# A hybrid encoder step: keys of two head groups, and the queries of one, projected turned, and rotated by a shuffle of partitions

## The chip, the cores and the metric

The kernel runs on one core of one Trainium2 chip. The metric is the time of one execution in device microseconds (us). Five instruction queues work side by side and meet by semaphores: TensorE (PE: matmuls and transposes, with weight loads shown as PEld), VectorE (DVE), ScalarE (ACT), GpSimd (POOL) and SyncE (SP, which issues the DMA transfers). SBUF and PSUM are the on-chip memories; PSUM's eight banks take what PE writes. Times are the median of several runs; a profile is one execution apart.

## The reference

One layer of a streaming encoder works on a prompt of 512 rows and on 32 new rows ("sample") of another sequence with caches. Rows are 1024 wide.

```
z = rmsnorm(x) @ w_in              # 3880 columns: qa ka va ga | qb kb vb gb | qm gm | qi ki wi
A: 6 heads x 64, attention over own chunk and 8 before, learned relative bias
B: 6 heads x 64, qb and kb rotated: [x1 cos - x2 sin, x2 cos + x1 sin] over halves of a head;
   an indexer (qi, ki, wi) picks the keys of each query, attention over those
M: 4 heads x 64, attention into 256 memory rows (their keys and values projected from mem)
x + concat(oA silu(ga), oB silu(gb), oM silu(gm)) @ w_out, then rmsnorm
```

Besides the two outputs, the new keys and values of A and B (prompt and sample), B's rotated indexer key and the memory's keys and values are returned. All is float32.

## The kernel before

Matmuls of 32-bit precision are made of three faster products: each operand is split into a high part, rounded (names ending in h: `xTh`, `wh`), and a low part, the rest (`xTl`, `wl`); high x high, low x high and high x low are summed in PSUM. The input stands turned in SBUF, model dimension on partitions, prompt and sample side by side (`xTh`, `xTl`: 8 pieces k of 128 x 544 columns).

Weights come in pieces by DMA (`raw`), ACT rounds a piece (`wh`) and POOL subtracts (`wl`). Two forms of projection use them. `group_n` ("natural") holds 128 rows of x as weights on PE and streams up to 384 columns of `wh`/`wl`: four row tiles, 8 k, 3 products; the result has rows on partitions. The 32 sample rows are not in it: `w_sample` computes them apart from the unsplit weights, eight matmuls of 32-row output for a projection, and `sample_rows` adds four partial sums on DVE. `group_t` ("turned") holds 128 weight columns and streams x in two halves of 272 columns (512 prompt rows and 32 sample rows); the result has features on partitions and needs no extra work for sample.

In the kernel before, A's keys (ka), A's values (va), B's keys (kb), queries (qb) and values (vb) are natural; A's queries, the memory's queries and the gates are turned. B's rotation is done on natural rows by `rope`: DVE multiplies by sine with the halves exchanged, DVE multiplies by cosine, DVE or POOL adds. Sample's rows get `rope_s`. Attention needs keys and queries turned: `turned_pair` transposes four 128 x 128 tiles on PE for a pair of heads, and `parts` splits the result into high and low. In `sample`, new keys are transposed and copied behind the cached ones.

The scores of a pair of heads and some row tiles form a unit: scores on PE, minimum and bias on DVE, exponential on ACT, normalization, transposes of the weights on PE (`turn`), and the product with the values (`mix`). A's and M's units come before B's.

The order of each engine's instructions is written when the program is built: a planner (`Line`) records every operation with an assumed cost, keeps a clock for each engine, and lets tasks issue when their inputs are due. PE's order is the backbone: the projections, in the order of `EARLY` and `LATE`, then the output projection; attention, sample and the selection of keys are put between their matmuls. All operations are recorded through one helper, so nearly every row of the profile has its line, L405. `SURE`, `LAG` and `SLACK` are the planner's margins and factor on costs; `WV` names the weight pieces that DVE splits in POOL's place. On SP, weights, caches, results stored and tables stand in one queue.

Of the kernel before, what the change touches and what calls it, by code (L numbers as in the profile page):

```python
# [10 lines left out]
F32 = mybir.dt.float32  # L11
# [9 lines left out]
T = 32  # L21
# [14 lines left out]
WV = (0, 1, 2, 3)  # L36
START = "xxxtwwwwrrrrrwmmrr"
SURE = 1.0
SLACK = 1.1
HOLD = 3.0  # L40
LAG = 0.2
# [3 lines left out]
EARLY = ("ka", "va", "mk", "mv", "qa0", "qa1", "ga0", "qa2", "ga1", "ga2", "qm0", "gm0", "qm1", "gm1")  # L45
LATE = ("gb0", "kb", "qb", "vb", "gb1", "gb2")
# [387 lines left out]
def hybrid_step(ctx: ExitStack, tc: tile.TileContext, a: dict):  # L434
# [73 lines left out]
    ka = va = ysS = None  # L508
# [69 lines left out]
    NATURAL = {"i": (QI, 296), "ka": (KA, 384), "va": (VA, 384), "kb": (KB, 384), "qb": (QB, 384), "vb": (VB, 384)}  # L578
    TURNED = {"qa": QA, "ga": GA, "qm": QM, "gm": GM, "gb": GB}
# [25 lines left out]
    def w_load():  # L605
        party = {p + j for _, p, _ in parties for j in range(NK // 2)} | set(range(n_in, n_in + 16))
        for i, (w, k, nk, lo, hi) in enumerate(w_list):
# [4 lines left out]
            if i == n_in + 12:  # L612

                yield from line.wait(lambda: units[-1].pair.q is not None)
# [87 lines left out]
    def sample_rows(nm, n, p):  # L702
        yield line.at(p)
        if nm in ("kb", "vb"):
            yield from line.wait(lambda: 0 in over)
        full = (cp.tile([P, 384], F32, tag={"kb": "kaS", "vb": "vaS"}.get(nm, nm + "S"), name=nm + "S") if nm != "i"
# [11 lines left out]
        yield from line.wait(lambda: NT in normed and (nm not in ("kb", "qb") or "qb" in over))  # L718
# [4 lines left out]
        if nm not in ("kb", "qb"):  # L723
            news[nm] = full if nm[0] == "v" else out
        if nm in ("kb", "qb"):
            yield from rope_s(out, T, 6, 64, ctab["cos64S"], ctab["sin64S"])
            news[nm] = out
# [219 lines left out]
    for nm in ("cos32", "sin32", "cos64", "sin64"):  # L947
        d = int(nm[3:])
        tp = ro if d == 64 else ix
        ctab[nm] = tp.tile([P, NT, d], F32, name=nm)  # L950
        ctab[nm + "S"] = tp.tile([T, d], F32, name=nm + "S")

    def load_tables(d):

        for nm in (f"cos{d}", f"sin{d}"):
            DMA.dma_start(ctab[nm], a[nm][0:S].rearrange("(t p) d -> p t d", p=P))
            DMA.dma_start(ctab[nm + "S"], a[nm][S:N])

        def scale():
            yield from line.wait(lambda: count["scored"] > 1)  # L960
            for t in range(NT):
                yield from line.wait(lambda: t in normed)
                for nm in (f"cos{d}", f"sin{d}"):
                    x = ctab[nm][:, t, :]
                    yield line.at(x, rs[:, t:t + 1])
                    G.tensor_scalar(x, x, rs[:, t:t + 1], None, op0=ALU.mult)
                over[d, t] = True

        if d == 64:
            line.spawn(scale())  # L970

    def rope(out, src, rows, nh, d, cos, sin, eng=None):
# [3 lines left out]
        t1 = ro.tile([P, 384], F32, tag="rt", name="rt")  # L976
# [8 lines left out]
    def rope_s(x, rows, nh, d, cos, sin):  # L985

        h2 = d // 2
        yield from room()
        p = bank()
        t1 = p[:rows, 0:nh * d]  # L990
        v2 = x.rearrange("p (h s d) -> p h s d", s=2, d=h2)[:, :, ::-1, :]
        sv = sin.rearrange("p (s d) -> p s d", s=2).unsqueeze(1).broadcast_to([rows, nh, 2, h2])
        yield line.idle(V)
        V.tensor_tensor(t1.rearrange("p (h s d) -> p h s d", s=2, d=h2), v2, sv, op=ALU.mult)
        yield line.idle(V)
        xv = x.rearrange("p (h d) -> p h d", d=d)
        V.tensor_tensor(xv, xv, cos.unsqueeze(1).broadcast_to([rows, nh, d]), op=ALU.mult)
        yield line.idle(V)
        V.tensor_tensor(x, t1, x, op=ALU.add)
        give(p)  # L1000


# [260 lines left out]
    def sample_choice():  # L1263
# [46 lines left out]
        yield from line.wait(lambda: count["scored"] >= len(TILES) and "qb" in over)  # L1310
# [38 lines left out]
    def project(nm, dst, out_p, out_s):  # L1349
        def done(t, acc):  # L1350
            if nm in ("kb", "qb"):
                rope(dst[:, t, :].rearrange("p (h d) -> p h d", d=64), acc[:, 0:384], P, 6, 64,
                     ctab["cos64"][:, t, :], ctab["sin64"][:, t, :])
            else:
                scaled(dst[:, t, :], acc[:, 0:384], rs[:, t:t + 1])

        def finish():
            if out_p:
                store_rows(a[out_p], dst)
                store_new(a[out_s], nm)  # L1360
            over[nm] = True

        return group_n(xTh, xTl, 384, NT, done, finish, 0, x_done)

# [55 lines left out]
    def projections(order):  # L1420
        nonlocal ka, va
        for nm in order:
            m = "abm".find(nm[1])
            if nm[0] in "qg" and nm != "qb" and gates[m] is None:
# [10 lines left out]
            elif nm[0] == "q" and nm != "qb":  # L1435
                line.until(lambda: "rb" in over)
                line.run(queries(nm))
            elif nm[0] == "m":
                line.run(memory(nm, mk if nm == "mk" else mv, f"new_mem_{nm[1]}_p"))
            else:  # L1440
                if nm not in natural:

                    line.until(lambda: NT - 1 in normed if nm[1] == "a" else (2 if nm == "kb" else 0) in over)
                    natural[nm] = cp.tile([P, NT, 384], F32, tag=nm, name=nm)
                    ka, va = (natural.get(n) for n in ("ka", "va"))
                of = f"new_{nm[1]}_{nm[0]}"
                line.run(project(nm, natural[nm], None if nm == "qb" else of + "_p", of + "_s"))


    def sample(mix, nh, nb, kt, cv, qT, kn, vn, pts, zin):  # L1450
# [5 lines left out]
        nk = nn + (T if kn is not None else 0)  # L1456
        if kn is not None:
            yield line.sure(kn)
            yield from room()
            p = bank()  # L1460
            for hp, k in enumerate(kt):
                PE.transpose(p[:, hp * T:(hp + 1) * T], kn[:, hp * P:(hp + 1) * P], ident[:T, :T])
            for hp, k in enumerate(kt):
                either(k[:, nn:nk], p[:, hp * T:(hp + 1) * T])
            give(p)
        yield line.sure(qT, *kt)
# [4 lines left out]
        for g0 in range(0, nh, 4):  # L1471
# [12 lines left out]
            def scores_of():  # L1484
                scs = [bank() for _ in cuts]
                for sc, (k0, n) in zip(scs, cuts):
                    for j, h in enumerate(hs):
                        r = 64 * (h % 2)
                        PE.matmul(sc[T * j:T * j + T, 0:n], qT[r:r + 64, h // 2, -T:], kt[h // 2][r:r + 64, k0:k0 + n],
# [131 lines left out]
    def sample_a():  # L1621
        yield from line.wait(lambda: all(n in over for n in ("qa0", "qa1", "qa2", "mk", "mv")) and "ka" in news and "va" in news)
        kt = cp.tile([P, 3, N], F32, tag="gate1", name="keysA")
        DMA.dma_start(kt[:, :, 0:S], a["cache_a_k"].rearrange("(m p) n -> p m n", p=P))
# [8 lines left out]
        yield from sample(0, 6, 4, [kt[:, m, :] for m in range(3)], cav, queried[0], news["ka"], news["va"],  # L1633
# [18 lines left out]
    def attention():  # L1652
        nonlocal ap, oax
        yield from line.wait(lambda: all(n in over for n in ("index", "index_s", "ka", "va")) and NT + NM // P in normed)
# [25 lines left out]
    def split_q(src, scale, sub):  # L1680
        return parts("q", src, S, scale, sub)

# [35 lines left out]

    SCORES = 9
# [163 lines left out]
    def biases():  # L1883
# [15 lines left out]
        yield from line.wait(lambda: count["mixed"] >= 3 * len(TILES))  # L1899
        oT[1] = cp.tile([P, 3, S], F32R, tag="ka", name="oBh"), cp.tile([P, 3, S], F32R, tag="va", name="oBl")  # L1900

    for hp in range(3):
        pair = Pair(0, hp, lambda hp=hp: both(split_q(queried[0][:, hp, 0:S], 1.0, G), keys_of(ka, hp)), lambda: va)
        pair.needs = lambda hp=hp: 2 * hp + 1 in nbs and f"qa{hp}" in over
# [221 lines left out]
```

## Time and profile before

| | |
|---|---|
| median of 3 runs (lowest to highest) | 352.41 us (352.28 to 352.43) |
| span of the profiled execution, first to last instruction | 350.8 us |
| PE busy | 342.6 us, 2748 matmuls |
| PE weight loads | 300.2 us |
| DVE / ACT / POOL busy | 277.5 / 224.2 / 174.3 us |
| mean granted TensorE clock | 0.996 |
| DMA | 46.31 MB |

A timeline row has the start in us, the duration in us, engine, line, operation, output<-inputs, shape, count and, in brackets, idle time before it with what ended it. Matmuls overlap in the pipeline, so a row's duration is longer than the step to the next row's start. Matmuls that read unsplit 32-bit data are recorded twice (x16 for 8). A row of groups has count | busy us, mean ns | idle time before and what ended it. A transfer's row has the count, KB each and median us from issue to landing.

### The profile page before, as it was taken

The page shows a single profiled execution, that of the slowest core. Times are in us where ns is not written, and L with a number is a line of the kernel's source. Part 1 is how long each engine was busy: PE and PEld are TensorE (multiplying, and loading weights), DVE is VectorE, ACT ScalarE, POOL GpSimd, SP SyncE. Part 2 cuts the span into 40 slices and gives each one's busy share as a digit, 9 for nine tenths or more (in the row PEclk, how much of TensorE's full clock was granted, in tenths as well). Part 3 has the DMA queues.
Part 4 walks back from the last instruction along what each step waited for, and adds up shares of the span by engine and source line. Part 5 has one row for each costly group of instructions (what it writes and reads, how often), then busy time and mean ns, then how long its engine had stood idle before and what let it go on. Part 6 is the DMA issues. An engine that isn't in the chain of part 4 may idle for free.

```text
span 350.8 us, 7580 instructions
## 1 busy us (share of the span) xinstructions
PE 342.6 (98%) x2748; PEld 300.2 (86%) x2748; DVE 277.5 (79%) x700; ACT 224.2 (64%) x536; POOL 174.3 (50%) x195
## 2 busy tenths in 40 slices
PE   8999999999999999999999999999999999999992
PEld 8979989989999998898898899899986777676882
DVE  3765768699889999997999945798996899674743
ACT  5759678898564876894757427413795786472542
POOL 3468264475554585255634473744471465215622
PEclk9999999999999999999999999999999999999998
DMA  7999542456538251343231232232372537300033
GB/s 230 323 360 354 134 140 75 143 162 152 151 92 296 66 144 39 78 127 88 76 91 45 93 124 58 60 93 98 95 284 92 180 106 265 114 0 2 0 111 143
DMA packets 39604, 46.31 MB, mean 132 GB/s; under 512 B 5360, under 2 KB 32624, under 8 KB 39568
## 3 DMA queue, kind: packets, MB, share of 16 engines
q1 hardware_dynamic: 39568, 45.85, 42.0%
q8 instruction: 21, 0.34, 0.4%
q14 instruction: 15, 0.12, 0.1%
HBM read 39.67 MB, written 6.16 MB: 131 GB/s over the span
## 4 chain that ended last, share of the span: by engine, by line
PE 95%; DVE 1%; ACT 1%; issue 1%; POOLq 0%; POOL 0%; ACTq 0%; DVEq 0%
PE bank L405 95%; DVE rot L405 1%; DVE xr L405 0%; ACT junkS L405 0%; DVE rt L405 0%; ACT wh L405 0%; ACT sq L405 0%; POOLq L2114 0%; POOL xr L405 0%; ACT bf_ok L405 0%; ACT k L405 0%; POOL ss L405 0%; ACT wI L405 0%; DVE ones L405 0%; ACTq L405 0%
## 5 line engine op out<-in xcount | busy, mean ns | idle before, releaser
L405 POOL TENSOR_TENSOR wl<-raw,wh 128x512 fp32r<-128x512 f32 (+1 forms) x69 | 104.5, 1523 | 79.9 <-ACT wh L405 68.2
L405 ACT ACTIVATE wh<-raw 128x512 fp32r<-128x512 f32 (+2 forms) x77 | 50.7, 662 | 23.4 <-PE bank L405 12.0
L405 PE MATMUL bank<-wh,xTh 128*128 128x384 f32 (+1 forms) x184 | 61.2, 347 | 0.2 <-ACT k L405 0.2
L405 PE MATMUL bank<-wl,xTh 128*128 128x384 f32 (+1 forms) x184 | 58.8, 334 | 0.0
L405 PE MATMUL bank<-wh,xTl 128*128 128x384 f32 (+1 forms) x184 | 58.5, 332 | 0.0
L405 ACT ACTIVATE z<-z,st 128x256 f32<-128x256 f32 (+3 forms) x80 | 42.4, 553 | 18.9 <-DVE st L405 18.7
L405 PE MATMUL bank<-xTh,wh 128*128 128x272 f32 x208 | 46.3, 303 | 0.0
L405 PE MATMUL bank<-xTl,wh 128*128 128x272 f32 x208 | 43.0, 288 | 0.0
L405 PE MATMUL bank<-xTh,wl 128*128 128x272 f32 x208 | 42.9, 288 | 0.0
L405 PEld LDWEIGHTS bank<-wh,xTh 128*128 128x128 f32 x184 | 34.1, 190 | 1.8 <-ACT wI L405 0.6
L405 PEld LDWEIGHTS bank<-xTh,wh 128*128 128x128 f32 x208 | 32.7, 189 | 2.7 <-issue 1.8
L405 PEld LDWEIGHTS bank<-wl,xTh 128*128 128x128 f32 x184 | 34.1, 190 | 0.0
L405 PEld LDWEIGHTS bank<-wh,xTl 128*128 128x128 f32 x184 | 33.9, 189 | 0.1
L405 PEld LDWEIGHTS bank<-xTl,wh 128*128 128x128 f32 x208 | 32.6, 188 | 0.0
L405 PEld LDWEIGHTS bank<-xTh,wl 128*128 128x128 f32 x208 | 32.6, 189 | 0.0
L405 DVE MAX8 m<-ysel 128x8 f32<-128x256 f32 (+2 forms) x48 | 26.5, 552 | 0.1
L405 DVE MATCH_REPLACE8 ysel<-m,ysel 128x256 f32<-128x256 f32 (+2 forms) x48 | 26.0, 542 | 0.0
L405 PE MATMUL bank<-ident,z 128*128 128x128 f32 (+1 forms) x162 | 24.8, 274 | 0.0
L405 ACT ACTIVATE junkS<-ysS,bi 128x1056 int8<-128x1056 f32 x16 | 18.8, 1172 | 6.8 <-DVE bi L405 5.7
L405 PEld LDWEIGHTS bank<-ident,z 128*128 128x128 f32 (+1 forms) x162 | 18.6, 140 | 5.1 <-issue 1.6
L405 ACT COPY z<-bank 128x512 f32<-128x512 f32 (+2 forms) x31 | 15.7, 520 | 10.2 <-PE bank L405 8.5
L405 DVE SCALAR_TENSOR_TENSOR ysel<-r,wI,ysel 128x256 f32<-128x256 f32 (+2 forms) x21 | 19.7, 938 | 2.4 <-ACT r L405 1.8
(299 smaller groups left out, 784.1 us busy)
## 6 DMA issues: line engine op xcount, KB each, us to landing
raw<-in_w_in_dram SPq DMA_DIRECT2D x20, 384.0 KB, 3.7
raw<-in_w_in_dram SPq DMA_DIRECT2D x26, 256.0 KB, 2.9
raw<-in_w_out_dram SPq DMA_DIRECT2D x16, 256.0 KB, 3.6
xr<-in_x_t_dram SPq DMA_DIRECT2D x8, 272.0 KB, 4.4
nat<-in_x_prompt_dram SPq DMA_DIRECT2D x4, 512.0 KB, 7.7
raw<-in_w_mem_kv_dram SPq DMA_DIRECT2D x8, 256.0 KB, 2.7
xr<-in_x_prompt_dram SPq DMA_DIRECT2D x4, 512.0 KB, 3.3
out_dram<-xr SPq DMA_DIRECT2D x4, 512.0 KB, 2.6
```

Source lines behind the costliest of these rows:

```text
L405: return fn(*args, **kw)
```

## The change

A's keys, B's keys and B's queries are projected turned, in three parts of 128 columns each (`ka0` to `ka2`, `kb0`, `qb0` and so on), prompt and sample together. `keys` takes a part out of PSUM: A's keys are multiplied by the rows' norms on DVE. B's go through `rope_t`: a shuffle within groups of 32 partitions exchanges the halves that a rotation mixes (the columns of `w_in` and the cached keys of B are put into the matching order on the host), DVE multiplies by cosine, DVE or POOL by sine, POOL adds. The tables of cosine and sine are now turned, 128 x 544, with the norms multiplied in on POOL. The transposes of ka, kb and qb, and those of sample's new keys and queries, are gone: `split_of` splits the turned tiles directly, and `sample` reads the new keys from their own tile. The extra matmuls for sample's rows remain for the indexer, va and vb. New keys are stored turned and put back by the host when it cuts the results apart. `EARLY` and `LATE` have a new order, and the planner's numbers differ.

```diff
-WV = (0, 1, 2, 3)
+WV = (0, 1, 2, 3, 5, 7)
-SURE = 1.0
-SLACK = 1.1
+SURE = 1.3
+SLACK = 1.05
-LAG = 0.2
+LAG = 0.3
-EARLY = ("ka", "va", "mk", "mv", "qa0", "qa1", "ga0", "qa2", "ga1", "ga2", "qm0", "gm0", "qm1", "gm1")
-LATE = ("gb0", "kb", "qb", "vb", "gb1", "gb2")
+EARLY = ("va", "ka0", "ka1", "mk", "ka2", "mv", "qa0", "qa1", "ga0", "qa2", "ga1", "ga2", "qm0", "gm0", "qm1", "gm1")
+LATE = ("gb0", "gb1", "gb2", "kb0", "qb0", "kb1", "qb1", "kb2", "qb2", "vb")
+SWAP = [(i + 16) % 32 for i in range(32)]
...
+    def rope_t(out, p, sl):
+        t = ro.tile([P, N // 2], F32, tag="rq", name="rq", bufs=2)
+        V.stream_shuffle(t, p, SWAP)
+        V.tensor_tensor(out, p, ctab["cos64"][:, sl], op=ALU.mult)
+        def rest():
+            least(out, V, G).tensor_tensor(t, t, ctab["sin64"][:, sl], op=ALU.mult)
+            yield line.at(t, out) - 0.2
+            G.tensor_tensor(out, t, out, op=ALU.add)
+        return rest()
...
+        def done(sl, p):
+            x = xT[:, i, sl]
+            if nm[1] == "b":
+                turned(x, p, sl)
             else:
+                V.tensor_tensor(x, p, rb[:, sl], op=ALU.mult)
+                ready(x)
+        return group_t(done)
...
-            for hp, k in enumerate(kt):
-                PE.transpose(p[:, hp * T:(hp + 1) * T], kn[:, hp * P:(hp + 1) * P], ident[:T, :T])
...
-        pair = Pair(1, hp, lambda hp=hp: both(turned_pair(natural["qb"], hp, lambda p, w: split_q(p, -0.125, V)), keys_of(natural["kb"], hp)),
+        pair = Pair(1, hp, lambda hp=hp: both(split_of(natural["qb"][:, hp, 0:S], -0.125, V, "q"),
+                                              split_of(natural["kb"][:, hp, 0:S], 1.0, G, "k")), lambda: natural["vb"])
```

Three places show how the order of instructions moves. First PE, where the first unit of B is prepared. Before (`ident,qb` and `ident,kb` are the transposes, `k,q` and its kin the scores, `xT` with `w` a turned projection, here of a gate):

```order
L405 MATMUL bank<-kl,q 128x256 x2
L405 MATMUL bank<-ident,qb 128x128 x4
L405 MATMUL bank<-ident,kb 128x128 x4
L405 MATMUL bank<-xTh_81,wh 128x272 x2
L405 MATMUL bank<-xTl_83,wh 128x272 x2
```

In the change the scores of that unit stand straight between the matmuls of a projection, which is now one of B's own keys and queries:

```order
L406 MATMUL bank<-xTh_82,wl 128x272 x2
L406 MATMUL bank<-k,q 128x128 x2
L406 MATMUL bank<-k,ql 128x128 x2
L406 MATMUL bank<-kl,q 128x128 x2
L406 MATMUL bank<-k,q 128x256 x2
L406 MATMUL bank<-k,ql 128x256 x2
L406 MATMUL bank<-kl,q 128x256 x2
L406 MATMUL bank<-xTh_82,wh 128x272 x2
```

The transposes are gone, and B's first scores have moved ahead of the end of B's projections.

Second POOL, in B's key and query parts. Before (`wl` is a weight split, `kb<-rt,kb` the last step of a rotation):

```order
L405 TENSOR_TENSOR ql<-queried,q 128x512
L405 TENSOR_TENSOR kb<-rt,kb 128x384
L405 TENSOR_TENSOR oAl<-o,oAh 128x384
L405 TENSOR_TENSOR kb<-rt,kb 128x384
L405 TENSOR_TENSOR wl<-raw,wh 128x768 x2
```

In the change (`rq` holds the shuffled half, `sin_123` the sine table, `kl` the low part of a pair's keys):

```order
L406 TENSOR_TENSOR wl<-raw,wh 128x512 x3
L406 TENSOR_TENSOR rq<-rq,sin_123 128x272
L406 TENSOR_TENSOR kb<-rq,kb 128x272
L406 TENSOR_TENSOR wl<-raw,wh 128x512
L406 TENSOR_TENSOR kb<-rq,kb 128x272
L406 TENSOR_TENSOR wl<-raw,wh 128x512
L406 TENSOR_TENSOR oMl<-o,oMh 128x512
L406 TENSOR_TENSOR wl<-raw,wh 128x512
L406 TENSOR_TENSOR rq<-rq,sin_123 128x272
L406 TENSOR_TENSOR qb<-rq,qb 128x272 x2
L406 TENSOR_TENSOR wl<-raw,wh 128x512
L406 TENSOR_TENSOR kl<-kb,k 128x512
```

The three splits in the first row are the second piece of `kb0` and both of `qb0`. All additions of the rotation, and sines, now stand between the weight splits of the following parts.

Third PE, where B's values, the last projection, end in the change (`oA`, `oM` belong to the output projection, `raw,oS` to sample's output, `z,vb` is the first product with B's values):

```order
L406 MATMUL bank<-wl,xTh_82 128x384
L406 MATMUL bank<-wh,oAh 128x512
L406 MATMUL bank<-wh,oAl 128x512
L406 MATMUL bank<-wl,oAh 128x512
...
L406 MATMUL bank<-wl,oMh 128x512
L406 MATMUL bank<-raw,oS 32x512 x4
L406 MATMUL bank<-z,vb 64x128 x6
```

Before, two gate projections stood between B's values and the output projection.

More of the change, by code (lines that the diff above doesn't have):

```diff
@@ L612, in w_load @@
             if i == n_in + 12:
-                yield from line.wait(lambda: units[-1].pair.q is not None)
+                yield from line.wait(lambda: units[-1].pair.q is not None and "newB" in over)
                 for tag, n, dtype in (("qb", 3, F32), ("kb", 2, F32R)):
@@ L717, in sample_rows @@
         give(p)
-        yield from line.wait(lambda: NT in normed and (nm not in ("kb", "qb") or "qb" in over))
+        yield from line.wait(lambda: NT in normed)
         yield max(line.at(rs[0:T, NT:NT + 1]), line.at(out) - 0.2)
@@ L722, in sample_rows @@
         V.tensor_scalar(out, out, rs[0:T, NT:NT + 1], None, op0=ALU.mult)
[L723 to L727, printed above, removed]
+        news[nm] = full if nm[0] == "v" else out
     def tokens(acc, xh, xl, w, c, t, c0, c1, first, last):
@@ L1455, in sample @@
         nn = nb * P
[L1456 to L1460, printed above, removed]
[L1461 to L1466 removed]
+        nk = nn + (T if vn is not None else 0)
+        yield line.sure(qT, *kt, *([kn] if kn is not None else []))
         yield from room(3)
@@ L1621, in sample_a @@
     def sample_a():
-        yield from line.wait(lambda: all(n in over for n in ("qa0", "qa1", "qa2", "mk", "mv")) and "ka" in news and "va" in news)
-        kt = cp.tile([P, 3, N], F32, tag="gate1", name="keysA")
-        DMA.dma_start(kt[:, :, 0:S], a["cache_a_k"].rearrange("(m p) n -> p m n", p=P))
+        yield from line.wait(lambda: all(n in over for n in ("qa0", "qa1", "qa2", "ka0", "ka1", "ka2", "mk", "mv")) and "va" in news)
+        kt = cp.tile([P, 3, S], F32, tag="gate1", name="keysA")
+        DMA.dma_start(kt, a["cache_a_k"].rearrange("(m p) n -> p m n", p=P))
         t = cp.tile([P, 3 * S], F32, tag="qb", name="tmpA")
@@ L1653, in attention @@
         nonlocal ap, oax
-        yield from line.wait(lambda: all(n in over for n in ("index", "index_s", "ka", "va")) and NT + NM // P in normed)
+        yield from line.wait(lambda: all(n in over for n in ("index", "index_s", "ka0", "va")) and NT + NM // P in normed)
         ipx.close()
@@ L1919, in hybrid_step @@
     projections(LATE)
-    line.until(lambda: 1 in gated and all(n in over and n in news for n in ("kb", "qb", "vb")))
+    line.until(lambda: 1 in gated and all(n in over for n in BK + ("vb",)) and "vb" in news)
     rox.close()
@@ L1951, in sample_b @@
         line.spawn(values())
-        yield from line.wait(lambda: "choice" in over and all(n in news for n in ("kb", "qb", "vb")))
+        yield from line.wait(lambda: "choice" in over and "vb" in news)
         z2 = cp.tile([P, NKS], F32, tag="rank", name="z2")
         V.tensor_copy(z2[0:2 * T], ysS[0:2 * T])
-        yield from room()
-        qbS = sp.tile([P, 3, T], F32, name="qbS")
-        p = bank()
-        for hp in range(3):
-            PE.transpose(p[:, hp * T:(hp + 1) * T], news["qb"][:, hp * P:(hp + 1) * P], ident[:T, :T])
-        rounded(qbS, p[:, 0:3 * T].rearrange("p (m c) -> p m c", m=3), -0.125)
-        give(p)
-        yield from sample(1, 6, 8, [t[:, 0:NKS] for t in kt], cbv, qbS, news["kb"], news["vb"],
-                          pts + [kt[2][:, NKS:]],
+        yield from sample(1, 6, 8, [t[:, 0:PAST] for t in kt], cbv, qbS, kbS, news["vb"],
+                          pts + [kt[2][:, PAST:]],
                           lambda g0, rows: z2 if g0 else ysS)
```

174 lines of the change are left out of this document (103 added, 71 removed).

## Prediction

> **What bounds the kernel now.** I read the page's busy shares first, then the chain that ended last, then what TensorE (PE) waited for.
>
> ```profile
> span 350.8 us, 7580 instructions
> PE 342.6 (98%) x2748; PEld 300.2 (86%) x2748; DVE 277.5 (79%) x700; ACT 224.2 (64%) x536; POOL 174.3 (50%) x195
> ...
> PE 95%; DVE 1%; ACT 1%; issue 1%; POOLq 0%; POOL 0%; ACTq 0%; DVEq 0%
> ...
> PE bank L405 <- DVE ones L405: 1.0, 1, 1.0
> PE bank L405 <- ACT bf_ok L405: 0.7, 1, 0.7
> PE bank L405 <- ACT k L405: 0.2, 1, 0.2
> ```
>
> The first line is one profiled execution; the median of the timed runs is 352.41 us, 1.6 us more, and I carry that difference over unchanged. PE is busy for 98% of the span, 95% of the last chain is PE, and PE's waits after the start come to 0.9 us. Busy PE is not PE at its peak, but with hardly a wait the spacing of its instructions is the time. So I price the change by start-to-start intervals on PE, and then ask whether the other engines still keep up.
>
> **The change part by part.**
>
> *Projections.* The timeline of PE, first and last row of a stretch of 384-wide matmuls with nothing between, then the same for 272-wide ones (a row of x2 is two matmuls with one weight tile):
>
> ```profile
> 33.12 0.34 PE L405 MATMUL bank<-wh,xTh 128*128 128x384 f32 x1
> ...
> 42.90 0.34 PE L405 MATMUL bank<-wl,xTh 128*128 128x384 f32 x1
> ...
> 247.30 0.42 PE L405 MATMUL bank<-xTl,wh 128*128 128x272 f32 x2
> ...
> 255.05 0.41 PE L405 MATMUL bank<-xTh,wl 128*128 128x272 f32 x2
> ```
>
> Between the first two lie 56 intervals: 9.78 / 56 = 0.1746 us each. Between the other two lie 62: 7.75 / 62 = 0.125 us. A projection of 384 columns was 4 row tiles x 8 k x 3 products = 96 matmuls, 16.76 us. Turned, with sample's 32 rows along, it is 3 parts x 8 k x 3 products x 2 halves = 144 matmuls, 18.0 us. Three projections turn (A's keys, B's keys, B's queries): **+3.72 us**.
>
> The Trainium skill, "TensorE: Matmul & The Clock Gate", section "Back-to-back issue gap", speaks against such a trade: it gives a sustained spacing of about 81 ns for 128 columns and 131 ns for 512, because weight load and matmul both count. On a straight line between these, an estimate, 272 columns take 100 ns and 384 take 114 ns, a projection goes from 11.0 to 14.4 us, and three cost +10.2 us in place of +3.72. The rows above disagree (125 and 174.6 ns) and are the very two shapes, so the measurement decides.
>
> *What goes from PE.*
>
> ```profile
> 44.16 1.50 PE L405 MATMUL bank<-raw,xF 128*32 128x384 f32 x16
> 45.58 0.82 PE L405 MATMUL bank<-identR,stk 32*128 32x32 f32 x8
> ...
> 126.82 0.66 PE L405 MATMUL bank<-ident,ka 128*128 128x128 f32 x4
> 127.23 0.50 PE L405 MATMUL bank<-xTh,wh 128*128 128x272 f32 x2
> ...
> 246.11 0.66 PE L405 MATMUL bank<-ident,qb 128*128 128x128 f32 x4
> 246.60 0.60 PE L405 MATMUL bank<-ident,kb 128*128 128x128 f32 x4
> 246.96 0.50 PE L405 MATMUL bank<-xTh,wh 128*128 128x272 f32 x2
> ...
> 260.44 0.37 PE L405 MATMUL bank<-ident,qbS 32*128 32x32 f32 x3
> 260.65 0.34 PE L405 MATMUL bank<-ident,kbS 32*128 32x32 f32 x3
> 260.93 0.50 PE L405 MATMUL bank<-wh,oAh 128*128 128x512 f32 x1
> ```
>
> Sample's own rows of a projection take 45.58 - 44.16 = 1.42 us; three such groups go: **-4.26**. A's keys are turned back in three groups of four transposes, 0.41 us each; B's queries and keys in three pairs of groups, 0.85 us a pair: 1.23 + 2.55 = **-3.78**. Sample's small transposes: 0.49 for B's two, half of it for A's keys: **-0.74**. The sample's scores against its 32 new keys stay as many and as wide; only their tile changes.
>
> *Re-entries.* A run of projections that starts again after something else is slow on its first step: 246.96 to 247.30 is 0.34 us where two matmuls take 0.25. The output projection does the same:
>
> ```profile
> 269.91 0.48 PE L405 MATMUL bank<-wh,oAh 128*128 128x512 f32 x1
> 270.23 0.40 PE L405 MATMUL bank<-wh,oAl 128*128 128x512 f32 x1
> 270.47 0.40 PE L405 MATMUL bank<-wl,oAh 128*128 128x512 f32 x1
> ```
>
> 0.32 against 0.24. Counted in the two orders of PE, projections and output projection stand in 105 runs before and in 90 now. At 0.09 us for each of 15: **-1.35**. It rests on the order alone, so its bounds are 0 and twice that.
>
> Sum on PE: 3.72 - 4.26 - 3.78 - 0.74 - 1.35 = **-6.4 us**; the span becomes 344.4, the median 346.0.
>
> *What it adds on DVE and POOL*, off PE's path if it arrives in time. No row shows the shuffle; the nearest below is a 272-wide product from PSUM, the nearest above an addition that had to wait:
>
> ```profile
> L405 DVE TENSOR_TENSOR gate<-bank,rb 128x272 f32<-128x272 f32 x16 | 6.2, 430 | 0.0
> L405 DVE TENSOR_TENSOR qb<-rt,qb 128x384 f32<-128x384 f32 x2 | 3.3, 1652 | 0.1
> L405 DVE TENSOR_TENSOR rt<-bank,sin 128x384 f32<-128x384 f32 x8 | 4.4, 556 | 3.6 <-POOL qb L405 2.2 <-POOL kb L405 1.1
> L405 POOL TENSOR_TENSOR gate<-tg,gate 128x272 f32<-128x272 f32 x9 | 7.3, 808 | 0.7
> L405 POOL TENSOR_TENSOR tg<-tg,gate 128x272 f32<-128x272 f32 x9 | 8.1, 898 | 5.8 <-ACT tg L405 5.8
> L405 POOL TENSOR_TENSOR wl<-raw,wh 128x512 fp32r<-128x512 f32 x49 | 65.8, 1351 | 61.1 <-ACT wh L405 51.0 <-PE bank L405 7.8 <-issue 1.4
> 178.00:258.00 80.00, 80.00 (x597) 74.42 (x596) 66.64 (x133) 41.74 (x102) 41.43 (x30) 1.00 0.30 91
> ```
>
> The last row (windows view: PE, PEld, DVE, ACT, POOL busy, clock, DMA share) is the stage of B's projections before: DVE 83% and POOL 52% busy, clock 1.00. I take 0.43 us for a shuffle (it reads PSUM and writes SBUF as that product does) and keep 1652 x 272/384 = 1.17 as the upper end. DVE then gains 12 shuffles and 12 products at 0.43 = 10.3 us and five sines of 0.43 to 1.17; it loses sixteen products of 0.55 (8.9 us), the two additions of the second row (3.3) and all steps on sample's rows of B's keys and queries. DVE gets no worse.
>
> One thing goes the other way: the low parts of A's keys and of B's queries were taken from PSUM and now have two inputs in SBUF. The rows show 1652 ns for an addition of two SBUF inputs against 556 for a product as wide from PSUM. The Trainium skill, "SBUF — State Buffer", section "Who interferes with whom", says why: DVE's second SBUF input comes through the read port it shares with POOL. By that rule each of six 512-wide steps may double or triple; the rows bear it out. They run ahead of the scores, not on PE's path.
>
> POOL gains, while the six B parts run, 12 additions (0.81), 7 sines (0.90) and two low parts of keys (1.35) = 18.7 us, beside 12 weight splits of 1.35 = 16.2 and two oM steps of about 1.4: 37.7 us. The six parts alone are 36 us of PE, and the attention pieces that stand among them stretch that further. So POOL is nearly full there, where it was half busy. What hides it: in POOL's new order both weight pieces of the next part stand ahead of a part's additions, so PE has a whole part, 6.0 us, to run before it needs the piece behind them. Without that cover each part would wait for the whole chain.
>
> SP gains six transfers (157 against 151). Weight pieces of 256 KB replace 384 KB in the early stage:
>
> ```profile
> raw<-in_w_in_dram SPq DMA_DIRECT2D x20, 384.0 KB, 3.7
> raw<-in_w_in_dram SPq DMA_DIRECT2D x26, 256.0 KB, 2.9
> ...
> 20.00:30.00 10.00, 9.83 (x60) 9.01 (x53) 6.22 (x18) 8.08 (x18) 5.53 (x12) 1.00 1.06 357
> ```
>
> Per KB the small piece lands 18% slower, and 20 to 30 us has all DMA engines full; but A's values, which keep the large pieces, now stand first, and the small pieces of A's keys are needed only one projection, 16.8 us, later. B's values are now projected last; twelve output-projection matmuls, 12 x 0.24 = 2.9 us, stand between them and the first product that reads them, against about 0.6 us for the last tile's eviction (the 384-wide row above); without that filling PE would wait those 0.6 us. The new numbers for margins and costs add no instruction. Two weight splits go from POOL to DVE early on. I add **+0.4 us** for waits that such a new order brings, an estimate from the 0.2 and 0.7 us waits it has now: **346.4 us**.
>
> **The rivals.**
>
> *The gain is partly eaten by late weights* (A's keys early, or one or two B parts). For: the full DMA stretch and POOL's load above. Against: PE's waits before name no weight at all. Six early pieces late by a fifth of 2.9 us are 3.5 us: 349.5.
>
> *Slower: the rotation holds POOL's queue, and weights come late at every B part.* Additions wait for two shuffles and two products on DVE, and the weight split behind them waits in line. Chain after a part's last matmul: 2 x 0.43 + 2 x 0.43 = 1.7, sine 0.9, two additions 1.6, split 1.35 = 5.6 us; with shuffles at 1.17 it is 7.0. Cover: 6.0 us. It decides from the point where five parts each lose 1.3 us, a chain of 7.3 us with nothing of attention in between. With a chain of 7.6 us the time is 346.0 + 5 x 1.6 = 354.0. For: DVE at 83%, and both engines' queues in series. Against: attention pieces stand in nearly every part.
>
> *No change.* By the skill's spacing of 100 and 114 ns, worked as a mechanism of this kernel (weight loads set PE's pace, so more matmuls cost more than fewer columns save), the projections lose 10.2 us, the sum is 10.2 - 10.1 = +0.1, the time 352.5. In rows: PEld is at 86%, but the 384-wide spacing exceeds the 272-wide one by the ratio 1.40 where the widths have 1.41, so width sets the pace, not loads.
>
> *More gain.* The two waits of 0.9 us vanish and the re-entries save twice as much: 344.2.
>
> **How the numbers follow.** Forecast 0.68; partly eaten 0.19; slower 0.06; no change 0.04; more 0.03. About 0.2% (0.7 us) is what a measurement can tell from no change. Faster by over that: 0.68 + 0.19 + 0.03 = 0.90; within 0.04; slower 0.06. The likeliest case has 345.0 to 347.8; the range goes down to 344.8 (waits gone and some re-entries more) and up to 350.2, past the eaten case; it leaves out the slower case, most of no change and a little at the low end.
>
> **What would show it.** In the profile after: PE's busy time near 336 us and still about 98%; 272-wide matmuls 0.125 us apart; no transposes of ka, kb or qb, two sample groups of 384 in place of five; shuffles near 0.43 us; PE's list of waits under 2 us. Wrong, if that list names DVE's or POOL's weight splits or additions with several us in the B parts, if PE falls well under 97%, or if the 272-wide spacing exceeds 0.13.

## The result, and the profile after

The changed kernel takes 350.52 us (median of 6 runs, 349.71 to 351.24) against 352.51 us before (352.28 to 353.47) on the same chip: a ratio of 0.9934, 95% interval 0.9914 to 0.9954. It is faster by 2.0 us where 6.0 were forecast, and 350.52 lies just above the upper end of the predicted range, 350.2.

The page of the changed kernel, its busy shares and its chain:

```profile
span 348.8 us, 7729 instructions
PE 338.3 (97%) x2799; PEld 298.6 (86%) x2799; DVE 280.2 (80%) x715; ACT 219.5 (63%) x522; POOL 191.1 (55%) x215
...
PE 85%; DVE 4%; ACT 4%; DMA 3%; issue 2%; POOL 1%; SPq 0%; POOLq 0%; DVEq 0%; ACTq 0%
```

And PE's list of waits (us in total, times, longest), complete:

```profile
PE bank L406 <- DMA raw<-in_w_out_dram: 1.5, 1, 1.5
PE bank L406 <- DVE ones L406: 1.0, 1, 1.0
PE bank L406 <- ACT z L406: 0.5, 1, 0.5
PE bank L406 <- POOL wl L406: 0.3, 1, 0.3
PE bank L406 <- DVE ka L406: 0.2, 1, 0.2
PE bank L406 <- ACT wh L406: 0.2, 1, 0.2
```

PE's busy time fell by 4.3 us, the span by 2.0. PE's chain share fell from 95 to 85%, and DVE, ACT, POOL and a DMA stand in the chain. A wait that before did not have heads the list: a piece of the output weights.

How much each kind of work costs PE is read from the steps between matmul starts, each step counted for the earlier matmul (my sum over the traces' records). First to last start is 343.22 us before (1.05 to 344.27) and 341.12 us after (1.05 to 342.17); behind the last matmul lie 6.5 and 6.6 us.

| PE, start to start | before, us | after, us | difference | forecast |
|---|---|---|---|---|
| projections of the model input (1176 and 1320 matmuls) | 180.86 | 184.56 | +3.70 | +3.72, less part of the re-entries |
| sample's own rows of projections (96 and 48) | 8.16 | 4.31 | -3.85 | -4.26 |
| transposes (243 and 198) | 24.26 | 20.79 | -3.47 | -4.52 |
| output projection (203 and 203 steps) | 47.96 | 46.94 | -1.02 | the rest of the re-entries' -1.35 |
| indexer scores of the prompt (24 and 24) | 5.52 | 4.67 | -0.85 | 0 |
| sample's output products (32 and 32) | 3.85 | 7.15 | **+3.31** | 0 |
| all the rest | | | +0.08 | waits, +0.4 |
| sum | 343.22 | 341.12 | -2.10 | -6.0 |

Without the row in bold the change would have saved 5.4 us on PE. The loss of that row is at one place. PE's timeline there, in the changed kernel:

```profile
267.93 0.49 PE L406 MATMUL bank<-wl,oMh 128*128 128x512 f32 x1
268.35 1.81 PE L406 MATMUL bank<-raw,oS 128*32 128x512 f32 x6
271.68 1.05 PE L406 MATMUL bank<-raw,oS 128*32 128x512 f32 x2 [1.52 <-DMA raw<-in_w_out_dram]
272.65 0.88 PE L406 MATMUL bank<-z,vb 128*64 128x128 f32 x12
```

Sample's second output product needs four weight pieces; its last matmul waits for the last piece. The wait shows as 1.52 us and the step across it as 2.11; besides, matmuls of this product that otherwise start 0.01 us apart now start up to 0.45 us apart, which makes up the 3.31. Why that is late, the chain in order of time says (start, duration, what):

```profile
254.97 10.29 PE bank L406 x60
...
265.28 0.58 ACT vb L406
...
266.09 1.79 POOL wl L406
267.88 0.02 issue
267.90 3.74 DMA raw<-in_w_out_dram
271.63 0.04 issue
271.68 67.99 PE bank L406 x540
```

The piece is issued only when a weight split on POOL has set a buffer free, and then takes 3.74 us to land. Around it, POOL's weight splits from 255 to 276 us and the two longest groups of DVE from 258 to 275 us:

```profile
L406 POOL TENSOR_TENSOR wl<-raw,wh 128x512 fp32r<-128x512 f32 x8 | 15.2, 1931 | 4.9 <-ACT wh L406 4.9
...
L406 DVE TENSOR_TENSOR_SCAN rank<-junkS 128x1056 f32<-128x1056 int8 x1 | 2.4, 2359 | 0.0
L406 DVE SCALAR_TENSOR_TENSOR rank<-rank,bf,junkS 128x1056 f32<-128x1056 f32 x1 | 2.2, 2153 | 0.0
```

And SP's queue in the timeline:

```profile
248.23 20.00 SPq L406 DMA_DIRECT2D raw<-in_w_out_dram  x7
268.27 1.60 SPq L406 DMA_DIRECT2D xr<-in_x_prompt_dram  x3
...
271.21 1.64 SPq L406 DMA_DIRECT2D keysB<-in_cache_b_k_dram  x3
```

A split takes 1.93 us here, 1.35 on average before. Seven loads hold SP's queue for 20 us, most of them waiting for a buffer that a split sets free, and the residual's rows (`xr`) and the cached keys wait behind them. In the kernel before SP had issued the same rows and keys from 254 us on:

```profile
244.23 6.29 SPq L405 DMA_DIRECT2D raw<-in_w_out_dram  x2
253.99 4.41 SPq L405 DMA_DIRECT2D xr<-in_x_prompt_dram  x3
258.45 1.38 SPq L405 DMA_DIRECT2D keysB<-in_cache_b_k_dram  x3
```

### The profile page after: what moved, and what is told of

It reads as the page before. It is cut to its first block, busy times and chain, and to the rows that moved or that the text cites. A ratio compares the mean times of both kernels' runs of the same rounds, so it can differ in the third digit from the quotient of the medians.

```text
span 348.8 us, 7729 instructions
## 1 busy us (share of the span) xinstructions
PE 338.3 (97%) x2799; PEld 298.6 (86%) x2799; DVE 280.2 (80%) x715; ACT 219.5 (63%) x522; POOL 191.1 (55%) x215
## 4 chain that ended last, share of the span: by engine, by line
PE 85%; DVE 4%; ACT 4%; DMA 3%; issue 2%; POOL 1%; SPq 0%; POOLq 0%; DVEq 0%; ACTq 0%
PE bank L406 85%; DMA nb<-in_bias_p_dram 1%; DVE ysel L406 1%; DMA raw<-in_w_out_dram 1%; DMA g_mix<-in_norm_mix_g_dram 1%; ACT z L406 1%; POOL wl L406 1%; ACT r L406 1%; DVE xr L406 0%; DVE m L406 0%; DVE gate L406 0%; ACT ysS L406 0%; ACT junkS L406 0%; DVE bi L406 0%; ACT QS L406 0%
## 5 line engine op out<-in xcount | busy, mean ns | idle before, releaser
L406 PE MATMUL bank<-xTh,wh 128*128 128x272 f32 x352 | 76.9, 300 | 0.0
L406 PE MATMUL bank<-xTh,wl 128*128 128x272 f32 x352 | 72.8, 288 | 0.3 <-POOL wl L406 0.3
L406 PE MATMUL bank<-xTl,wh 128*128 128x272 f32 x352 | 72.7, 288 | 0.0
L406 PEld LDWEIGHTS bank<-xTh,wh 128*128 128x128 f32 x352 | 55.1, 189 | 3.3 <-issue 2.7
L406 PEld LDWEIGHTS bank<-xTh,wl 128*128 128x128 f32 x352 | 55.0, 189 | 0.5 <-POOL wl L406 0.5
L406 PEld LDWEIGHTS bank<-xTl,wh 128*128 128x128 f32 x352 | 55.3, 188 | 0.0
L406 PE MATMUL bank<-wh,xTh 128*128 128x384 f32 (+1 forms) x88 | 27.0, 336 | 0.2 <-ACT wh L406 0.2
L406 PE MATMUL bank<-wl,xTh 128*128 128x384 f32 (+1 forms) x88 | 26.3, 328 | 0.1
L406 PE MATMUL bank<-wh,xTl 128*128 128x384 f32 (+1 forms) x88 | 26.2, 327 | 0.0
L406 DVE TENSOR_SCALAR z<-z,st 128x256 f32<-128x256 f32 (+3 forms) x32 | 17.6, 590 | 0.6
```

The lines of the kernel that those rows point to most:

```text
L406: return fn(*args, **kw)
```

## The experiments

Four theories were set against each other. **Contention**: wide DVE steps of sample's key selection slow POOL's splits, so the piece starts late. **Transfers**: the transfers, or the product's place right behind the last projection, make it late whatever POOL does. **Supply**: output weights are short over the whole stretch, and a wait that is taken away comes back. **Numbers**: the 2 us come from the planner's numbers and not from the turned projections.

### The wait taken away in two ways

First, four wide steps of DVE made narrow; the planner is told the old cost of each (`line.planned`), and the order of every engine is as in the changed kernel. What the four steps compute for sample's selection is left out.

```diff
-        V.tensor_tensor_scan(rank, junkS, junkS, 0.0, op0=ALU.add, op1=ALU.max)
+        line.planned = NKS; V.tensor_tensor_scan(rank[:, 0:8], junkS[:, 0:8], junkS[:, 0:8], 0.0, op0=ALU.add, op1=ALU.max)
...
```

> The changed kernel, in which four wide DVE steps at the end of sample's selection (the running sum, two products of two SBUF inputs and one masked step, 1056 columns each) work on 8 columns, with the times that the order was made by kept, so that every engine's order stays as it is; what they compute is left out. Contention (DVE's wide steps slow POOL's weight splits, so that the last output piece for sample's second product starts late): the seven splits from 260 us take about 1.3 us each in place of 1.97, the piece is issued at least 3 us earlier, PE's wait at that product goes, and the time falls by 2.5 to 3.3 us to 347.2 to 348.0. Transfers late by themselves: the splits may get faster, but the product waits as before, time within 0.7 us of 350.5. Supply short overall: the wait at the product goes, and at least 1.5 us of it come back at later pieces or at the cached keys: 349.0 to 350.0.

Measured: 348.89 us (348.14 to 350.44), ratio 0.9885 (0.9847 to 0.9922), span 346.4. POOL's splits from 255 to 276 us in this run:

```profile
L406 POOL TENSOR_TENSOR wl<-raw,wh 128x512 fp32r<-128x512 f32 x8 | 10.2, 1300 | 7.4 <-ACT wh L406 7.4
```

And PE's timeline at the product:

```profile
269.31 1.04 PE L406 MATMUL bank<-raw,oS 128*32 128x512 f32 x2 [0.54 <-DMA raw<-in_w_out_dram]
```

The splits fall from 1.93 to 1.30 us with nothing changed but DVE's four steps, and the wait from 1.52 to 0.54. By the sum of steps, sample's output products still cost 5.42 us, 1.57 over before in place of 3.31. So contention is real and carries about half of the loss. The Trainium skill, "SBUF — State Buffer", section "Who interferes with whom", has the rule: a DVE instruction with two inputs in SBUF contends with a GpSimd instruction that reads SBUF. The trace agrees, with 1.93 against 1.30 us. What stays is the transfer: the piece is issued 3.75 us earlier (264.15 against 267.90), but four pieces are now issued within 1.4 us, and it takes 5.12 us to land in place of 3.74. The time is above the forecast 347.2 to 348.0. The span fell by 2.4 us, but this profile is the fastest of the four executions; by the medians the time fell by 1.6.

Second, the late piece read by nobody at the product, which makes the second of sample's output products another one:

```diff
-                        PE.matmul(p[q * T:(q + 1) * T, :], oS[:, kt, :], raws[i0 + 4 * j + q][:, 0, :],
+                        PE.matmul(p[q * T:(q + 1) * T, :], oS[:, kt, :], raws[i0 + 4 * j + (min(q, 2) if at_ == 4 else q)][:, 0, :],
```

> The changed kernel, in which the last of the four weight pieces of sample's second output product is replaced by the piece before it (one operand; the order of every engine stays as it is; the product is then another one). The late piece is then read by nobody until its split. If that one piece is the whole loss of about 3 us: the gap of 2.1 us at the product goes, PE waits on no output piece, time 347.5 to 348.5. If the supply is short overall: the same microseconds return within the next 15 us, at other output pieces or at the cached keys that queue behind them on SP: 349.5 to 350.5.

Measured: 348.73 us (347.89 to 348.80), ratio 0.9869 (0.9839 to 0.9899), span 346.1. PE's list names only the start and 0.3 us of POOL; the sum of sample's output products is 4.24 us, 0.39 over before. First to last start is 338.48 us, 2.6 less than in the changed kernel, in the fastest of four executions. From the last projection matmul to the last matmul of all PE takes 75.13 us in place of 77.26, so of the 2.9 us won at the product 2.1 are kept and at most 0.8 came back later. That speaks against supply, for this place, and shows the late piece as nearly the whole loss there. The time is 0.2 us above the forecast 347.5 to 348.5.

### The product moved

```diff
-            yield line.sure(oS, *raws[i0:i0 + k])
+            yield line.sure(oS, *raws[i0:i0 + k]) + (4.0 if at_ == 4 else 0.0)
```

> The changed kernel, but sample's second output product may be issued only 4 us after its weights are due by the planner; nothing is left out. Theories C and T both: it stands 55 matmuls behind the last projection in place of 13, PE's gap of 2.6 us goes, time 347.8 to 348.8. Rival S (the supply of output weights is short as a whole): the gap turns up again at a later matmul that reads such a weight, time 350 to 351.

Measured: 349.26 us (348.57 to 349.99), ratio 0.9899 (0.988 to 0.9917), span 347.5. The wait at the product is gone, but in the new order PE waits 0.44 and 0.24 us for cached keys, which SP issued behind the output pieces:

```profile
279.28 1.05 PE L406 MATMUL bank<-keysB,qbS 64*32 64x512 f32 x4 [0.44 <-DMA keysB<-in_cache_b_k_dram]
280.57 1.48 PE L406 MATMUL bank<-keysB,qbS 64*32 64x512 f32 x10 [0.24 <-DMA keysB<-in_cache_b_k_dram]
```

First to last start is 339.82 us, 1.3 less than in the changed kernel, where 3.3 had gone from the product; from the last projection matmul on it is 76.13 us, 1.1 less. So most of the loss came back, as the supply theory has it; in this order, not in the one above. The time lies between the two forecasts.

With 1.0 in place of 4.0, only six output matmuls move ahead of the product:

> The changed kernel with sample's second output product held back by 1 us in the plan: on PE only six output matmuls (1.4 us) move ahead of it, SP's and POOL's orders stay as they are. If the loss is the wait for one late piece: the wait of 1.5 us for it falls to about 0.2, nothing queues later on SP, time 348.8 to 349.3 (1.3 to 1.6 us less than the changed kernel). If the supply is short overall: the six matmuls need pieces that POOL has not split yet, PE waits for those, time 350.0 or more.

Measured: 349.65 us (347.95 to 351.00), ratio 0.9904 (0.988 to 0.9928), span 349.2. The excess of sample's output products fell from 3.31 to 0.89 us, and PE's list names no output piece any more. From the last projection matmul to the last matmul PE takes 76.26 us, so only 1.0 of the 2.4 us won is kept. The time is a little over the forecast. The profiled execution is the slowest of the six: sample's first output product starts at 263.36 us against 261.88, though up to there the order is the same, and 1.8 us of delay were there before 20 us. One order thus differs by 1.5 us from execution to execution, which a profile alone does not tell from an effect. The sums from the last projection matmul on leave this early difference out.

### The selection moved

```diff
-        yield from line.wait(lambda: count["scored"] >= len(TILES) and "qb2" in over)
+        yield from line.wait(lambda: count["scored"] >= len(TILES) and "qb0" in over)
```

> The changed kernel, but the last steps of sample's selection on DVE may start once the first query part of B is out (qb0), not the last (qb2); nothing is left out. Theory C (contention): in the changed kernel POOL's burst of output-weight splits takes 1.97 us each beside these DVE steps in place of 1.35, so the last weight piece that sample's second output product reads is fetched late, and PE stands still for about 2.6 us at 269 us. With the steps earlier the splits of that burst fall to 1.5 us or less, PE's gap there to under 0.7 us, and the time to 347.9 to 348.9. Rival T (the transfers themselves are late, because that product stands only 13 matmuls after the last projection): splits get faster, the gap stays at 2 us or more, time 350 to 351.

Measured: 351.53 us (median of 12 runs; 11 from 350.16 to 353.41, and one of 823.83 us, without which the median is 351.36), ratio 0.9977 (0.9958 to 0.9997), span 349.0. Its splits from 255 to 276 us:

```profile
L406 POOL TENSOR_TENSOR wl<-raw,wh 128x512 fp32r<-128x512 f32 x8 | 10.1, 1291 | 6.9 <-ACT wh L406 6.7
```

And PE's list of waits:

```profile
PE bank L406 <- ACT z L406: 2.0, 1, 2.0
PE bank L406 <- DVE ones L406: 1.0, 1, 1.0
PE bank L406 <- POOL wl L406: 0.6, 1, 0.6
PE bank L406 <- ACT wh L406: 0.5, 1, 0.5
PE bank L406 <- DMA raw<-in_w_out_dram: 0.2, 1, 0.2
```

The splits are fast (1.29 us) and the wait for the piece falls to 0.2 (by the sum of steps 1.25 us are left at sample's output products), but the wide steps now stand ahead of an attention step, and PE waits 2.0 us for that one. The wait was moved, not removed, and the time is above both forecasts. With "qb1", one part earlier in place of two:

> The changed kernel with the end of sample's selection one part earlier, and nothing else. In PE's order sample's second output product stands where it stood in the changed kernel, 17 output matmuls or so behind the last projection. If the place of the product is what counts: the late piece comes about 1.4 us earlier, as with the 1 us beside it, so 1 to 2 us of the wait stay, time 348.8 to 350.0. If the earlier selection alone carries the gain: no wait on an output piece, time 347.2 to 348.2.

Measured: 348.60 us (348.33 to 349.46), ratio 0.988 (0.9862 to 0.9899), span 347.7. Sample's output products cost 4.50 us, 0.65 over before, and no wait of 2 us appears. The time is just under the first forecast and above the second: the earlier selection takes away most of the loss, and the rest stays at the product. Contention is not what it takes away, for the splits from 255 to 276 us still take 1.92 us each. They start earlier: POOL's idle time before them falls from 4.9 to 1.2 us, and the last of the seven pieces is issued 1.5 us behind the last projection matmul in place of 3.0.

### Both moved

"qb1" with the product held back by 4 us:

> The changed kernel with the end of sample's selection started one part earlier (after the second of B's query parts) and sample's second output product held back by 4 us. If contention and the early product are two causes that add: the splits in the burst take 1.3 to 1.5 us, no wait on an output piece, time 347.5 to 348.8. If the supply is short overall: about 349.3, as with the delay alone. If an attention step on DVE is held up instead (as with the selection two parts earlier, a wait of 2.0 us): 349.5 to 351.5.

Measured: 349.54 us (348.26 to 350.62), ratio 0.9896 (0.9858 to 0.9933), span 347.6. The splits take 1.93 us, not the 1.3 to 1.5 that the first theory asked for. PE's list names nothing but the start and 0.3 us; first to last start is 337.85 us, 5.4 less than before. But behind the last matmul lie 8.7 us. Sample's third product came at 332 us (PE's timeline, 324 us in the changed kernel):

```profile
332.15 1.92 PE L406 MATMUL bank<-raw,oS 128*32 128x512 f32 x16
```

and behind it come eight additions to sample's residual on DVE, about 0.69 us each, on the chain that ends last; two of them:

```profile
335.45 0.70 DVE xrS L406
...
338.53 0.68 DVE xrS L406
```

"qb1" with 1 us:

> The changed kernel with the end of sample's selection one part earlier and sample's second output product held back by 1 us. The run with 4 us had PE's first to last start at 337.8 us, 5.4 less than before, but 8.7 us behind the last matmul in place of 6.6, because sample's third output product came at 332 us. Here that product stands 26 rows earlier in PE's order. If that was the cause of the longer end: PE 337.8 to 338.8 us and an end of 6.6 to 7.0 us, a span of 345.5 to 346.9 and a time of 347.2 to 348.6. If the end stays long: 349 to 350.

Measured: **347.40 us** (347.25 to 347.97), ratio 0.9851 (0.9836 to 0.9867): 5.3 us faster than before, and faster than the changed kernel, whose interval (0.9914 to 0.9954) lies apart. The span is 345.5 us; its busy shares:

```profile
PE 336.7 (97%) x2799; PEld 299.1 (87%) x2799; DVE 280.2 (81%) x714; ACT 218.1 (63%) x522; POOL 192.3 (56%) x216
```

PE's waits, complete:

```profile
PE bank L406 <- DVE ones L406: 1.0, 1, 1.0
PE bank L406 <- POOL wl L406: 0.5, 1, 0.5
```

POOL's splits from 255 to 276 us:

```profile
L406 POOL TENSOR_TENSOR wl<-raw,wh 128x512 fp32r<-128x512 f32 x8 | 15.3, 1934 | 1.1 <-ACT wh L406 1.1
```

And the product in PE's timeline:

```profile
272.25 1.06 PE L406 MATMUL bank<-raw,oS 128*32 128x512 f32 x8
```

First to last start is 337.09 us, 6.1 less than before, with 7.4 us behind the last matmul. The time lies at the lower end of the forecast by two misses that cancel in part: PE's part is 0.7 us under its range, the end 0.4 us over. The splits are as slow as in the changed kernel (1.93 us): contention was not cured here. But the product starts 7.7 us behind the last projection matmul (264.59) in place of 3.5 (264.90 to 268.35), and SP is through with the seven loads at 266.4 us in place of 268.2, so no matmul waits for the slow splits.

### The numbers apart from the turned projections

The changed kernel with the old `SURE`, `SLACK`, `LAG` and `WV`:

```diff
-WV = (0, 1, 2, 3, 5, 7)
-SURE = 1.3
-SLACK = 1.05
+WV = (0, 1, 2, 3)
+SURE = 1.0
+SLACK = 1.1
...
-LAG = 0.3
+LAG = 0.2
```

> The changed kernel with the planner's numbers and the list of DVE's splits of the kernel before (margins 1.0 and 0.2, cost factor 1.1, splits 0 to 3); nothing is left out. Theory C or T: PE's work is the same within 0.1 us by the order, sample's second output product stands 69 matmuls after the last projection, so that gap is gone; with tighter margins other short waits come in its place; 348 to 350. Rival N (the gain came from the numbers, the turned projections give nothing): 352 to 353.

Measured: 350.72 us (350.17 to 353.36), ratio 0.9948 (0.9924 to 0.9972). That cannot be told from the changed kernel, though the order is another, and it lies between the two forecasts. Here too PE waits for an output piece, 1.2 us, although sample's second output product now starts 13.3 us behind the last projection matmul. In this order the piece stands in SP's queue behind the residual's rows and the cached keys; it is issued at 273.5 us and lands 9.1 us later. So distance alone is no cure, and here the transfers make the piece late. And the kernel before with the new three margins:

```diff
-SURE = 1.0
-SLACK = 1.1
+SURE = 1.3
+SLACK = 1.05
...
-LAG = 0.2
+LAG = 0.3
```

> The kernel before with the new margins and cost factor alone (1.3, 0.3, 1.05), projections natural as they were; nothing is left out. By the order of PE, fewer restarts save 0.9 us. Theory C or T: 351.5 to 352.7. Rival N: 350.5, as the change.

Measured: 371.79 us (369.93 to 372.49), ratio 1.053 (1.0505 to 1.0555). So the numbers theory falls: the gain is that of the turned projections together with their order (`EARLY`, `LATE`); no run tells these two apart. That the margins alone cost 19 us in the old kernel was in neither forecast. PE's first to last start grew by 12.1 us, and the end behind it from 6.5 to 13.3 us. The last matmul of this run:

```profile
355.04 1.92 PE L405 MATMUL bank<-raw,oS 128*32 128x512 f32 x16
```

And two windows (PE, PEld, DVE, ACT, POOL busy, clock, DMA share, GB/s):

```profile
40.00:45.00 5.00, 5.00 (x25) 4.88 (x24) 4.89 (x12) 4.96 (x11) 2.53 (x2) 0.66 0.00 0
...
270.00:275.00 5.00, 5.00 (x35) 3.35 (x34) 4.96 (x10) 3.94 (x11) 2.04 (x2) 0.72 0.01 3
```

Sample's third product is PE's very last work, and its additions follow on DVE. By the steps between starts, two gaps of 2.2 and 2.6 us stand before these windows, each followed by a lower granted clock. These and the longer end account for part of the 19 us; the rest was not traced.

### The gates behind B's values again

```diff
-LATE = ("gb0", "gb1", "gb2", "kb0", "qb0", "kb1", "qb1", "kb2", "qb2", "vb")
+LATE = ("gb0", "kb0", "qb0", "kb1", "qb1", "kb2", "qb2", "vb", "gb1", "gb2")
```

> The changed kernel with two of B's three gate parts behind B's values again, as before the change. Cover lost (the 12 us of gate projections that stood between B's values and the output stage gave SP and POOL time for output pieces, the residual's rows and the cached keys): output pieces and the cached keys are issued while projections still run, PE's list of waits names no output piece and no cached keys, time 346.5 to 348.0. Rival, that any order of this planner loses 2 to 3 us somewhere: PE waits 2 us or more elsewhere, time 349.5 to 351.5.

Measured: 360.38 us (359.66 to 360.58), ratio 1.0197 (1.0161 to 1.0234), span 358.8. PE waits on no output piece and no cached keys, as the cover theory said, but the time was far off for both. A new wait of 2.6 us (for `cacheM`, by ACT) appears, and sample's third product comes at 343.05 us, at PE's end, with 14 us behind it. Whether the old place of the gates would help with a good end stays open: this order changes too much at once.

## Why the prediction was right or wrong

**What bounds the kernel: right.** PE was busy for 98% and still is for 97%. What PE's start-to-start sum leaves out is the end behind the last matmul, 6.5 and 6.6 us here; it grew to 13.3 and 14.4 us in the two slow orders.

**Projections, +3.72: right, and the last digit is luck.** The median step of the 272-wide ones is 0.125 us, as before, over 1000 steps. The sum of +3.70 also holds two waits of 0.3 and 0.5 us and has a few restarts less; in the experiments with the turned projections the same 1320 matmuls took 183.4 to 186.4 us, +2.5 to +5.5. The rival by weight-load spacing ("no change", 352.5) is refuted by that median.

**Sample's groups, -4.26, and transposes, -3.78 and -0.74: right for what went, short by 0.4 and 1.0 in the sums.** Measured -3.85 and -3.47. The 45 transposes that went had cost 4.49 us before, against 4.52 forecast, and a group of sample's rows 1.40 to 1.46. What stayed grew dearer. The group of A's values takes 1.86 us at 18.5 us in the changed kernel. The transposes left cost 20.79 / 198 = 0.105 us each in place of 24.26 / 243 = 0.100. Part of that is the way of counting: a step from a transpose to another takes 0.110 and 0.111 us before and after, a step from a transpose to other work only 0.064 and 0.076, and of these there are 33 in place of 55, because the transposes now stand in longer runs.

**Re-entries, -1.35: right in kind.** The output projection stands in 13 runs in place of 24 and gave -1.02, about 0.09 us for each of the 11; the projections' part (64 runs in place of 68) cannot be separated from their sum.

**The sum on PE, -6.4: too large by 1.8.** The four rows that I had priced (projections, sample's rows, transposes, output projection) give -4.6, and all but the first fall short. The changed kernel shows -5.4 without the one wait only because the indexer's scores gave -0.85, whose wait of 0.7 us I had put into a rival. The -6.1 with the selection one part earlier and the product 1 us later holds -0.96 from there too.

**The failed step: "I add +0.4 us for waits that such a new order brings".** Sample's output products alone took 3.31 us more, nearly all of it at one product that waited for a weight piece. Of the 3.9 us between -6.0 and the measured -2.10 this term is 3.0 (3.31 and 0.08 in place of 0.4); the priced terms' 1.8 us, less the indexer's 0.85, make up the rest. Two sentences of mine had the parts and did not join them. I wrote that two-input steps on DVE slow down beside POOL, "not on PE's path", and looked only at DVE's side, and only at the new steps: POOL's splits slow down as well, beside steps of the selection that were there before, and they set weight buffers free. And I counted the cover behind B's values for the product that reads the values (twelve output matmuls, 2.9 us) and not for the next one in line, sample's output product, which reads weights. That the gates had left this place, so that output pieces, the residual's rows and the cached keys all came due at once, stood in the order that I quoted.

**The rivals.** "Partly eaten by late weights" (349.5, chance 0.19) was right in kind and in sign, 1 us short in size, and wrong in place: PE's list has no wait for a weight in A's keys or in B's parts, only one of 0.3 us for a split at 113.7 us, and the loss is at the output weights. "Slower, the rotation holds POOL's queue" did not come: from 178 to 258 us PE is busy without a break. That window of the changed kernel (PE, PEld, DVE, ACT, POOL busy, clock, DMA share, GB/s), and behind it the new steps of DVE in groups:

```profile
178.00:258.00 80.00, 80.00 (x701) 75.75 (x701) 66.76 (x157) 42.54 (x114) 54.99 (x53) 1.00 0.30 82
```

```profile
L406 DVE STREAM_SHUFFLE rq<-bank 128x272 f32<-128x272 f32 x12 | 5.7, 471 | 0.0
L406 DVE TENSOR_TENSOR rq<-rq,sin 128x272 f32<-128x272 f32 x5 | 6.2, 1241 | 0.0
L406 DVE SCALAR_TENSOR_TENSOR ql<-qb,q 128x512 fp32r<-128x512 f32 x3 | 4.7, 1570 | 0.2 <-ACT q L406 0.2
L406 DVE TENSOR_TENSOR kl<-ka,k 128x512 fp32r<-128x512 f32 x3 | 2.8, 925 | 0.0
```

POOL's busy time rose from 41.43 to 54.99 of these 80 us, 69%; I had it "nearly full", and it still left room. The shuffle takes 0.47 us where I took 0.43. A sine on DVE takes 1.24 us, past my upper end of 1.17. The low parts of B's queries take 1.57 us and those of A's keys 0.93, against 0.68 for both before; none of them shows in PE's waits.

**The list of what would show it.** PE busy 338.3 in place of 336, waits 3.7 us in place of under 2: the second told at once that the +0.4 was the term. The other signs came as written: 0.125 us between 272-wide matmuls, a PE share of 97%, and no wait of several us in the B parts.

## What to carry to other kernels

When work leaves a full engine, price what stays and then ask, for each wait that can now end last, when its input was issued and what sets its buffer free; follow that back through the engines that are "off the path". An engine with 55% load can still be the one that frees the buffers, and a wide two-input step elsewhere stretches its operations by half. Where a planner writes the order, look at the places where one queue's transfers meet one product before trusting a sum: here one condition and 1 us of delay were worth another 3 us.

## What the runs showed that I had not expected

The slowing is large, and the rows show the later of two overlapping steps paying for it. On the mean a split on POOL took 1.93 us beside DVE's wide steps and 1.30 without them; one took 3.37. In the changed kernel:

```profile
260.48 3.37 POOL L406 TENSOR_TENSOR wl<-raw,wh 128x512 fp32r<-128x512 f32 x1 [2.79 <-ACT wh L406]
262.81 2.15 DVE L406 SCALAR_TENSOR_TENSOR rank<-rank,bf,junkS 128x1056 f32<-128x1056 f32 x1
```

And in the kernel before:

```profile
251.34 1.31 DVE L405 SCALAR_TENSOR_TENSOR rank<-rank,bf,junkS 128x1056 f32<-128x1056 f32 x1
251.51 2.29 POOL L405 TENSOR_TENSOR wl<-raw,wh 128x512 fp32r<-128x512 f32 x1 [1.36 <-ACT wh L405]
```

DVE's masked product of 1056 columns took 2.15 us where it started inside a running split, and 1.31 where it started first and the split took 2.29. DVE's running sum started at 260.41 us, just ahead of the split of 3.37 us, and took 2.36 us against 2.35 in the kernel before. With the four steps narrow, the masked product of only 8 columns still took 1.15 us at 260.39 us, up to the end of a split that had started at 260.23. These rows fit a later step that waits for the earlier one's end; no run was made to test it.

The granted clock does not follow the length of a gap alone. Gaps of 2.24 and 2.56 us on PE were followed by 5 us windows at 0.66 and 0.72, while a gap of 2.31 us (selection two parts early, at 242 us) left 1.00 in its window and the next, and the changed kernel's 2.1 us at 269.6 and the 2.83 us at 180.7 with the gates last left 1.00 too. The Trainium skill, "TensorE: Matmul & The Clock Gate", section "What's actually happening", puts the lower clock down to an idle window of about 3.4 us that runs freely; the gaps here are all shorter than that, and two of them lowered the clock, so the measurement decides. What tells these gaps apart stays open.

And small edits of the planner's numbers or order moved the time by up to 19 us, most visibly when sample's third output product slid to PE's end, where eight additions of 0.69 us follow on DVE.
